# Group softmax on one core: tiles of 256 rows in six buffers, and hardware loops on VectorE and ScalarE

## The chip, the core and the metric

The kernel runs on one core of one Trainium2 chip. The metric is the device time of one execution in microseconds; lower is better. A profiled execution has a span (first to last instruction on the core) and its own time, which is a little longer.

## The reference

```python
def setup_inputs():
    B, N, D, G = 4, 4096, 4352, 8
    return {"x": np.random.randn(B, N, D).astype(np.float32)}

def reference(x):
    B, N, D = x.shape
    G = 8
    Dg = D // G
    x_g = x.reshape(B, N, G, Dg)
    x_g = x_g - x_g.max(axis=-1, keepdims=True)
    exp = np.exp(x_g)
    out = exp / exp.sum(axis=-1, keepdims=True)
    return out.reshape(B, N, D).astype(np.float32)
```

There are 16384 rows of 4352 floats. Each row is eight groups of 544, and each group gets a softmax of its own. 285 MB are read and 285 MB are written.

## The kernel before

A tile is 128 rows, one per SBUF partition, so a partition holds one row of 17408 bytes. There are 128 tiles and a pool of 12 buffers for them (`NBUF`), and everything is done in place in the buffer.

For each tile, `load` (L37) brings it in with one transfer. `expo` takes the negated maximum of all eight groups with one VectorE reduction (L45) and then runs eight ScalarE activations (L49), one per group, each of which writes exp(x - max) and leaves the group's sum. `scale` takes the reciprocals of the eight sums on VectorE (L61) and multiplies the groups with eight VectorE instructions (L63). `store` (L40) writes the tile out with one transfer.

Both kinds of transfer are issued from the SP queue[...]. The program is written out in full: there is no loop on the chip. The order is set by hand (`manual_schedule`). Ten loads are issued first (`AHEAD` is 10). Then, in step i, `expo(i)` is followed by `scale(i-1)`, `store(i-1)` and `load(i+9)`. So on VectorE the maximum of a tile stands ahead of the scaling of the tile before it. A load takes the buffer of the tile that was stored two steps earlier and waits until that store has landed. The waits between engines are placed by the Tile layer.

## Time and profile before

| | |
|---|---|
| median of 10 runs | 1341.88 us (1340.17 to 1342.72) |
| profiled execution, its own time | 1341.4 us |
| its span | 1339.6 us |
| VectorE busy | 1046.6 us (78%) |
| ScalarE busy | 764.4 us (57%) |
| moved by DMA | 570.70 MB, 426 GB/s over the span |

The profile is one execution taken by the hardware profiler. Its busy times show how much of the span an engine worked; its slices show when. The DMA lines give the mean busy share of the core's 16 DMA engines and what they moved together[...]. Queue q1 carries the kernel's loads and stores, q14 the fetching of instructions. "Landing" is when all 16 engines have reported that their share of a transfer is done.

### The profile page before, as it was taken

The numbers are of one execution on the slowest core, as the hardware profiler recorded it, in microseconds if no ns is written. First come the engines' busy times: TensorE is split into PE (matmuls) and PEld (weight loads), VectorE is DVE, ScalarE is ACT, GpSimd is POOL, SyncE is SP. The second block draws the span as 40 slices with busy tenths as digits, with TensorE's granted clock in tenths as the row PEclk, the third lists the DMA queues.
The fourth block names the chain that finished last, engine by engine and source line by source line (L and its number), as shares of the span: only waits on it lengthen the run. The fifth ranks groups of instructions, "written<-read, shape, count | busy, mean of one in ns | idle before, by whom it ended". The sixth has DMA issues, their size and how long they took to land.

```text
span 1339.6 us, 4119 instructions
## 1 busy us (share of the span) xinstructions
DVE 1046.6 (78%) x1280; ACT 764.4 (57%) x2049; POOL 0.2 (0%) x4
## 2 busy tenths in 40 slices
DVE  6999987878777877888777777778877887778760
ACT  5777766556655565556555555655555555655540
POOL 0000000000000000000000000000000000000000
DMA  9999999999999999999999999999999999999996
GB/s 399 427 429 428 431 431 432 431 430 431 432 431 430 432 431 431 431 431 431 431 430 430 431 430 431 430 431 431 431 431 430 432 431 432 430 431 431 431 431 272
DMA packets 36896, 570.70 MB, mean 426 GB/s; under 512 B 4096, under 2 KB 4096, under 8 KB 4096
## 3 DMA queue, kind: packets, MB, share of 16 engines
q1 hardware_dynamic: 36864, 570.44, 99.5%
q14 instruction: 32, 0.26, 0.0%
HBM read 285.21 MB, written 285.21 MB: 426 GB/s over the span
## 4 chain that ended last, share of the span: by engine, by line
DMA 93%; DVE 1%; SPq 1%; ACT 1%; issue 1%; DVEq 0%; ACTq 0%
DMA out_dram<-xt 91%; DMA xt<-in_x_dram 3%; SPq L37 1%; ACT xt L49 1%; DVE xt L63 1%; DVE mx L45 1%; DVE rs L61 0%; DVEq L104 0%; ACTq L104 0%
## 5 line engine op out<-in xcount | busy, mean ns | idle before, releaser
L49 ACT ACTIVATE xt<-xt,mx 128x544 f32<-128x544 f32 x1024 | 751.2, 734 | 524.1 <-issue 427.5
L45 DVE TENSOR_REDUCE mx<-xt 128x8 f32<-128x4352 f32 x128 | 599.7, 4685 | 247.2 <-DMA xt<-in_x_dram 247.1
L63 DVE TENSOR_SCALAR xt<-xt,rs 128x544 f32<-128x544 f32 x1024 | 434.1, 498 | 4.5
L49 ACT ACTIVATION_READ_ACCUMULATOR xt<-xt,mx 128x1 f32 x1024 | 191.1, 187 | 0.0
L61 DVE RECIPROCAL rs<-sm 128x8 f32<-128x8 f32 x128 | 24.7, 193 | 3.4 <-ACT xt L49 3.4
L49 ACT ACT_TABLE_LOAD x1 | 1.3, 1283 | 9.5 <-DMA xt<-in_x_dram 9.5
L93 POOL MEMSET const-bfloat16-1.0<- 128x1 bf16 x1 | 0.1, 102 | 0.0
L93 POOL MEMSET const-uint8-127<- 128x1 uint8 x1 | 0.1, 101 | 0.0
L93 POOL MEMSET const-float32-0.0<- 128x1 f32 x1 | 0.1, 99 | 0.2 <-issue 0.2
L93 POOL MEMSET const-float32-1.0<- 128x1 f32 x1 | 0.1, 98 | 0.0
## 6 DMA issues: line engine op xcount, KB each, us to landing
xt<-in_x_dram SPq DMA_DIRECT2D x128, 2176.0 KB, 25.8
out_dram<-xt SPq DMA_DIRECT2D x128, 2176.0 KB, 30.8
```

Source lines behind the costliest of these rows:

```text
L37: nc.sync.dma_start(out=xt, in_=xg[i * P:(i + 1) * P])
L45: nc.vector.reduce_max(out=mx, in_=xt, axis=mybir.AxisListType.X, negate=True)
L49: nc.scalar.activation(out=xt[:, g, :], in_=xt[:, g, :], func=mybir.ActivationFunctionType.Exp, bias=mx[:, g:g + 1], scale=1.0, accum_out= ...
L61: nc.vector.reciprocal(out=rs, in_=sums.pop(i))
L63: nc.vector.tensor_scalar_mul(out=xt[:, g, :], in0=xt[:, g, :], scalar1=rs[:, g:g + 1])
L93: nc = _bacc.Bacc("TRN2", target_bir_lowering=False, num_devices=1)
```

## The change

A tile is now 256 rows, two adjacent rows per partition (`R = 2`), so a partition's share of a transfer is one contiguous piece of 34816 bytes. There are 64 tiles in six buffers of twice the size (`NT = 6`), the same memory as before. Compute still works on 128 rows at a time, now called a row slot s of twelve (`S`): two slots per buffer, each with its own place in `mx`, `sm` and `rs`.

SP issues five loads and then alternates `store(t)` and `load(t+5)`. A load waits until the store that last used its buffer has landed. The Tile layer no longer places the waits: the kernel has semaphores of its own, `landed` and `stored` per buffer, and `max_done`, `exp_done`, `rec_done` and `scaled` across the engines. VectorE waits for its own reciprocal by `rec_done`.

VectorE and ScalarE run a hardware loop each, over a body of twelve row slots, ten turns, and the last eight row groups are written out behind it. [...] The order on VectorE is still: the maximum of the next row group, then the scaling of this one. SP's program stays written out.

```diff
-    NBUF = 12
+    R = 2
+    NT = 6
+    S = R * NT
-    nt = N // P
+    nt = N // (P * R)
+    nr = nt * R
+    turns = (nr - 1) // S
+    xt = xf.rearrange("(t p r) d -> t p (r d)", p=P, r=R)
+    ot = of.rearrange("(t p r) d -> t p (r d)", p=P, r=R)
-    pool = ctx.enter_context(tc.tile_pool(name="io", bufs=NBUF))
-    small = ctx.enter_context(tc.tile_pool(name="small", bufs=4))
+    ctx.enter_context(tc.tile_critical(no_gpsimd_drain=True))
+    ctx.enter_context(nc.cleanup_on_exit())
+    bufs = [ctx.enter_context(nc.sbuf_tensor(f"xt{b}", [P, R * D], f32)) for b in range(NT)]
...
+    def vector_max(s):
+        if s % R == 0:
+            nc.vector.sem_inc(landed[s // R], -16).wait_op(landed[s // R], 16, "sem-ge")
+        nc.vector.reduce_max(out=mx[:, s, :], in_=row(s), axis=X, negate=True).then_inc(max_done, 1)
+    def vector_scale(s):
+        nc.vector.sem_inc(exp_done, -1).wait_op(exp_done, 1, "sem-ge")
+        nc.vector.reciprocal(out=rs[:, s, :], in_=sm[:, s, :]).then_inc(rec_done, 1)
+        nc.vector.sem_inc(rec_done, -1).wait_op(rec_done, 1, "sem-ge")
+        xr = row(s)
         for g in range(G):
+            i = nc.vector.tensor_scalar_mul(
+                out=xr[:, g, :], in0=xr[:, g, :], scalar1=rs[:, s, g:g + 1])
+        i.then_inc(scaled, 1)
+    def scalar_exp(s):
+        nc.scalar.sem_inc(max_done, -1).wait_op(max_done, 1, "sem-ge")
...
+        i.then_inc(exp_done, 1)
+    def loop(engine):
+        return nc.Fori(
+            0, turns, engines=OrderedEngineSet([engine.engine]), head_slot={engine.engine: 0})
+    with nc.Block(no_gpsimd_drain=True) as block:
+        @block.sync
+        def _(sync):
+            def load(t):
+                b = t % NT
+                if t >= NT:
+                    sync.wait_ge(stored[b], 16 * (t // NT))
+                sync.dma_start(out=bufs[b][:, :], in_=xt[t]).then_inc(landed[b], 16)
-    AHEAD = NBUF - 2
-    with tc.manual_schedule():
-        for i in range(AHEAD):
-            load(i)
-        for i in range(nt + 1):
-            if i < nt:
-                expo(i)
-            if i:
-                scale(i - 1)
-                store(i - 1, nc.sync)
-                if i - 1 + AHEAD < nt:
-                    load(i - 1 + AHEAD)
+            for t in range(NT - 1):
+                load(t)
+            for t in range(nt):
+                sync.wait_ge(scaled, R * (t + 1))
+                sync.dma_start(out=ot[t], in_=bufs[t % NT][:, :]).then_inc(stored[t % NT], 16)
+                if t + NT - 1 < nt:
+                    load(t + NT - 1)
+            for b in range(NT):
+                sync.wait_ge(stored[b], 16 * ((nt - b + NT - 1) // NT))
+        @block.vector
+        def _(vector):
+            vector_max(0)
+            with loop(vector):
+                for s in range(S):
+                    vector_max((s + 1) % S)
+                    vector_scale(s)
+            for n in range(turns * S, nr):
+                if n + 1 < nr:
+                    vector_max((n + 1) % S)
+                vector_scale(n % S)
+        @block.scalar
+        def _(scalar):
+            scalar.preload_act_table(Exp)
+            with loop(scalar):
+                for s in range(S):
+                    scalar_exp(s)
+            for n in range(turns * S, nr):
+                scalar_exp(n % S)
```

## The prediction

> **What bounds the kernel now.** I read the busy line and the slices first, then the DMA queues, the chain that ended last, the groups, and last the end of the run in short windows.

> ```profile
> DVE 1046.6 (78%) x1280; ACT 764.4 (57%) x2049; POOL 0.2 (0%) x4
> ...
> DMA  9999999999999999999999999999999999999996
> GB/s 399 427 429 428 431 431 432 431 430 431 432 431 430 432 431 431 431 431 431 431 430 430 431 430 431 430 431 431 431 431 430 432 431 432 430 431 431 431 431 272
> ...
> q1 hardware_dynamic: 36864, 570.44, 99.5%
> q14 instruction: 32, 0.26, 0.0%
> ...
> DMA 93%; DVE 1%; SPq 1%; ACT 1%; issue 1%; DVEq 0%; ACTq 0%
> ```

> No compute engine is above 78%, the 16 DMA engines are full in every slice but the last, and the chain is 93% DMA. So only what makes the transfers shorter, or evens them out, moves the end. Compute has room: a row group (128 rows) costs VectorE 4.685 + 0.193 + 8 x 0.424 (434.1 us over 1024) = 8.27 us, while a load and a store of it take two transfers of 5.17 us.

> The last slice, 272 GB/s, is where the unevenness shows (columns: stretch, busy time of each engine, clock, DMA share, GB/s):

> ```profile
> 1316.00:1320.00 4.00, 0.00 (x0) 0.00 (x0) 0.00 (x0) 1.00 1.02 440
> 1320.00:1322.00 2.00, 0.00 (x0) 0.00 (x0) 0.00 (x0) 1.00 0.97 418
> 1322.00:1324.00 2.00, 0.00 (x0) 0.00 (x0) 0.00 (x0) 1.00 0.97 418
> 1324.00:1326.00 2.00, 0.00 (x0) 0.00 (x0) 0.00 (x0) 1.00 0.53 226
> 1326.00:1328.00 2.00, 0.00 (x0) 0.00 (x0) 0.00 (x0) 1.00 0.26 113
> ...
> 1332.00:1334.00 2.00, 0.00 (x0) 0.00 (x0) 0.00 (x0) 1.00 0.20 87
> 1334.00:1336.00 2.00, 0.00 (x0) 0.00 (x0) 0.00 (x0) 1.00 0.14 61
> 1336.00:1338.00 2.00, 0.00 (x0) 0.00 (x0) 0.00 (x0) 1.00 0.12 52
> ```

> One engine moves 431/16 = 27 GB/s. So all 16 work until 1324, about four at 1327, two at 1337. **The end is set by the slowest two of 16 DMA engines, some 13 us after most had finished.** The trace's completion records (one per engine and transfer) agree: of the last transfer's 16, twelve come 13.1 to 13.7 us before the last one, one 9.8, one 3.6, one 0.2. I call this distance an engine's lag. From those records the two last engines' lag grows in steps of 0.6 to 0.8 us, and most of these steps come where the packet records have one of the 28 instruction fetches (8192 bytes each) that fall inside the span: at 643.8 us one fetch, and the last lag goes from 5.8 to 6.5 us. The chain shows the same thing from outside:

> ```profile
> 478.47 30.54 DMA out_dram<-xt
> ...
> 509.40 31.55 DMA out_dram<-xt
> ...
> 541.40 30.51 DMA out_dram<-xt
> ```

> The middle piece holds two fetches, at 519.0 and 522.8 us; its neighbours hold none. Not every fetch shows (one at 450.5 fell on an engine that was not last). The two lags sum to about 27 us; 28 fetches x 0.7 = 19.6 us of it. The other 7 us come in the first 170 us and between 700 and 820 us, beside slow packets with no fetch. A third engine (9.8 us) drifts by about 0.03 us per transfer with no steps until late; I have no cause for it.

> [...] In the packet records a 17408-byte packet [...] starts 645 ns after the one before it: an overhead of 5 ns[...]. [...]

> **The change, part by part.**

> *Packets.* An engine now does, per transfer, 8 packets and a semaphore write of 9 ns: 8 x 645 + 9 = 5169 ns, x 256 = 1323.3 us (most engines in fact run from 1.75 to 1325 us). With 34816 bytes: 8 x (1280 + 5) + 9 = 10289 ns, x 128 = 1317.0 us. Saved: 6.3 us, all on the path. Bounds: 0 if the 5 ns grow with the size or the descriptor is split; 6.3 us if all of it is fixed. The jitter above 645 I leave as it is.

> *Loops.* The program goes from 1404 to 273 instructions on VectorE, from 1277 to 204 on ScalarE (2301 and 364 with the accumulator read that follows each activation) and from 398 to 155 on SP. A loop body is 152 on VectorE (12 x (1 maximum, 1 reciprocal, 8 multiplies, 2.5 waits) and the branch) and 206 on ScalarE (12 x (16 + 1 wait), and the branch). [...] so no turn should fetch. The 273 + 364 + 155 and padding are 8 to 12 fetches, mostly ahead of the first load. So of the two lags of 13.1 to 13.7 us, some 3.5 us should stay (7 us over two engines). Then the third engine is last. Its 9.8 us stay if its drift goes with bytes, and are about 5 if with packets. I take 8 us. Bounds: 3.5 (its drift gone) and 13.7 (the lag isn't the fetches). Gain 5.7 us.

> *Waits and order.* SP's queue keeps its form. load(i+5) waits for store(i-1); behind that in the ring stand load(i+4) and store(i), 2 x 10.3 us, as 4 x 5.17 us before, so an engine may lead the slowest by some 18 us before it idles; lags are below that. store(i) waits until two row groups are scaled: the second's scaling stands behind the maximum of the next tile, so it is done 4.7 + 3.6 us after load(i+1) landed; six transfers (62 us) lie between that landing and the store's place in the ring. Covered. The maximum now waits for 4.4 MB, 5.1 us more, once, at the start; five loads (51 us) are queued behind it and the first store is ready at about 14.6 + 2 x 4.7 + 7.4 + 3.4 + 3.4 = 38 us. Covered. At the end 4 stores (41 us) stand between the last landing and the last store's turn, less the lag 8; compute needs 8.3 + 4.7 + 7.4 + 3.6 = 24 us. Covered by 9 us. The own semaphores and VectorE's wait for its own reciprocal: 128 x 2.5 small instructions, none shown in the trace; at even 0.2 us each, 0.5 us per row group, they fit in VectorE's 10.3 - 8.3 = 2 us; if that cover were gone, stores would be late first. The ten branches fall there too. Bounds 0 and 2 us; I take 0.

> *Entry and exit.* One more block with its barriers, semaphore clearing: the trace has its own (first load at 0.73 us, end 0.8 us after the last landing). I take 1.6 us for a second such pair; bounds 0.5 and 4.

> **Sum** against the profiled run (span 1339.6, 1341.4 us in all): -6.3 - 5.7 + 1.6 = -10.4, so 1331.0. The median of the runs, 1341.88, is 0.5 above it: **1331.5 us**.

> **Rivals.** (a) Lag cut, packets no cheaper: 1337.8. For it: the 5 ns is small and measured only at one size. (b) Packets cheaper, lag stays since its cause is not the fetches (the stretch at 700 to 820 us speaks for that): 1341.9 - 6.3 + 1.6 = 1337.2. (c) *Slower:* the loops fetch their body again on every turn, so the change does not do what its loops are for. Two packets [...] per engine and turn are 40, with the straight code 48 fetches. At 13.5/28 us of lag each that is 23 us instead of 13.5, and the time is 1337.2 + 9.6 = 1346.8. It decides from 13.5 + 4.7 = 18.2 us of lag, or 38 fetches; there the faster engines begin to idle as well. [...] (d) Other losses: 34 KB packets slower than two of 17 KB, or a ring that runs dry at the coarser steps. If one engine in each transfer waits 0.1 us it is 128 x 0.1 = 13 us: 1344 and above. Nothing in the profile speaks for it.

> **How the numbers follow.** A measurement of this kernel can tell about 0.2% (2.7 us). Both parts work: 0.46, 1327 to 1336; with the third engine's drift gone too, 0.06, 1324 to 1327. (a) 0.13, (b) 0.09, both 1334 to 1339. No change that can be told: 0.08. (c) 0.09. (d) 0.09. Faster 0.74, same 0.08, slower 0.18. A range of 1325 to 1343 leaves out (c), (d) and a little at the low end. The likeliest case's own range is 1327 to 1336.

> **What would show it.** q14 with 12 packets or fewer, and q1 with half of its 36864; GB/s of 432 to 433 in the middle slices, where it was 431; a tail in short windows that goes from full rate to nothing in 8 us or less rather than 13; VectorE and ScalarE busy times unchanged; SP waiting for stores, not for VectorE. Wrong, if q14 has as many packets as before, if the middle slices stay at 431, or if a stretch shows the DMA share below 0.95 before the tail.

## The result and the profile after

The changed kernel takes **1331.11 us** (median of 8 runs, 1330.15 to 1332.69), the kernel before 1341.53 us (28 runs beside it). The ratio is 0.9923, 95% interval 0.9915 to 0.9932: 10.4 us faster. The forecast was 1331.5 us, and most of its steps held, but two of its terms were off in opposite directions, so that the total came out better than its parts.

From the page of the kernel after, the lines that answer to those of before:

```profile
span 1328.9 us, 4036 instructions
...
DVE 1041.4 (78%) x1280; ACT 764.5 (58%) x2049; POOL 0.2 (0%) x4
...
DMA  9999999999999999999999999999999999999997
GB/s 401 419 433 435 433 433 430 431 434 433 435 434 429 433 432 435 435 435 434 429 434 432 435 435 434 431 433 432 434 436 436 432 430 434 433 434 436 433 431 329
...
q1 hardware_dynamic: 18432, 570.43, 99.6%
q14 instruction: 9, 0.07, 0.0%
...
DVE 0%; DVEq 0%; issue 0%
```

VectorE and ScalarE do the same work in the same time. Half of the packets on q1 are gone, q14 has 9 packets where it had 32, the middle slices went from about 431 to about 433 GB/s (means of 200 us: 432 to 434, with a DMA share of 1.00 or 1.01), and the last slice from 272 to 329. The chain (last line) can no longer be read: with the kernel's own semaphores it stops after the last multiplications, so there is nothing to set beside the chain's pieces of before.

The end of the kernel after, in short windows (stretch, busy times, clock, DMA share, GB/s):

```profile
1316.00:1318.00 2.00, 0.00 (x0) 0.00 (x0) 0.00 (x0) 1.00 1.09 470
1318.00:1320.00 2.00, 0.00 (x0) 0.00 (x0) 0.00 (x0) 1.00 0.77 331
1320.00:1322.00 2.00, 0.00 (x0) 0.00 (x0) 0.00 (x0) 1.00 0.32 139
1322.00:1324.00 2.00, 0.00 (x0) 0.00 (x0) 0.00 (x0) 1.00 0.24 104
1324.00:1326.00 2.00, 0.00 (x0) 0.00 (x0) 0.00 (x0) 1.00 0.08 35
```

Before, the bulk of the engines stopped at 1324 to 1326 us and the last two went on to 1338. Now the bulk stops at 1319 to 1321 and the last at 1326. (A window's rate can exceed what the engines move, since a packet of 1.3 us is counted where it falls.) So both parts of the forecast can be seen in one view: every engine has less to do, and the spread between the engines is smaller.

To part the two in every run I take from the trace's completion records of the last transfer when the sixth of its 16 engines was done ("bulk"), and how much later the last one was ("lag"). These records carry the time of each completion and not the name of the engine, so an engine can be followed only by how far it is behind.

| kernel | time, us | ratio to before, 95% interval | bulk ends | lag | q14 packets |
|---|---|---|---|---|---|
| before | 1341.5 | | 1325.4 | 13.5 | 32 |
| after | 1331.1 | 0.9923 (0.9915 to 0.9932) | 1320.5 | 5.9 | 9 |
| e1: loops written out | 1340.6 | 0.9993 (0.9984 to 1.0001) | 1320.7 | 16.3 | 31 |
| e2: one row per partition | 1334.7 | 0.9951 (0.9937 to 0.9965) | 1325.5 | 4.9 | 10 |
| e3: both undone | 1344.0 | 1.0018 (1.0009 to 1.0026) | 1325.5 | 14.5 | 32 |
| e4: two rows, two packets | 1334.9 | 0.9953 (0.9940 to 0.9967) | 1325.0 | 5.6 | 9 |
| e5: ScalarE written out | 1336.8 | 0.9968 (0.9957 to 0.9980) | 1320.5 | 11.8 | 22 |
| e6: bodies of 24 | 1352.9 | 1.0081 (1.0068 to 1.0094) | 1323.7 | 16.8 | 32 |
| e7: bodies of 48 | 1345.4 | 1.0028 (1.0010 to 1.0045) | 1326.0 | 16.8 | 36 |
| e8: three rows | 1328.5 | 0.9901 (0.9887 to 0.9915) | 1319.0 | 5.5 | 8 |
| e9: bodies of 24, deeper ring | 1345.7 | 1.0028 (1.0017 to 1.0038) | 1335.4 | 6.4 | 33 |
| e10: transfers alone | 1330.5 | 0.9919 (0.9906 to 0.9933) | 1321.1 | 4.3 | 1 |

Bulk, lag and packets come from each kernel's one profiled execution, the times from its runs.

### The profile page after: what moved, and what is told of

Its sections match the earlier page's. It is cut to its first block, busy times and chain, and to the rows that moved or that the text cites. A ratio compares the mean times of both kernels' runs of the same rounds, so it can differ in the third digit from the quotient of the medians.

```text
span 1328.9 us, 4036 instructions
## 1 busy us (share of the span) xinstructions
DVE 1041.4 (78%) x1280; ACT 764.5 (58%) x2049; POOL 0.2 (0%) x4
## 2 busy tenths in 40 slices
DMA packets 18441, 570.51 MB, mean 429 GB/s; under 512 B 2048, under 2 KB 2048, under 8 KB 2048
```

## The experiments

### e1 to e4: each part undone

e1 writes the loops out:

```diff
-            with loop(vector):
-                for s in range(S):
-                    vector_max((s + 1) % S)
-                    vector_scale(s)
-            for n in range(turns * S, nr):
+            for n in range(nr):
                 if n + 1 < nr:
...
-            with loop(scalar):
-                for s in range(S):
-                    scalar_exp(s)
-            for n in range(turns * S, nr):
+            for n in range(nr):
                 scalar_exp(n % S)
```

> The changed kernel (1331.1 us) with its two hardware loops written out, packets of 34816 bytes kept. Theory (fetches make the lag): about 31 packets on q14 instead of 9, the last two engines' lag goes from 6 back to about 13.5 us, the packet step stays 1285 ns: 1331.1 + 7.5 = 1338.6 us. Rival (the smaller lag comes from fewer packets or transfers, not from fewer fetches): lag stays at 6 us and the time at 1331 to 1332 us.

e2 keeps the loops and goes back to one row per partition:

```diff
-    R = 2
-    NT = 6
+    R = 1
+    NT = 12
+    AHEAD = NT - 2
...
-            for t in range(NT - 1):
+            for t in range(AHEAD):
...
-                if t + NT - 1 < nt:
-                    load(t + NT - 1)
+                if t + AHEAD < nt:
+                    load(t + AHEAD)
```

> The changed kernel with its loops kept and one row per partition: 128 transfers each way of 17408-byte packets, twelve buffers, ten loads ahead as in the kernel before. Theory (a fixed 5 ns per packet and 9 ns per transfer and engine): packet step 645 ns, 6.3 us more work on every engine, lag 6 us: 1337.4 us. Rival (the whole gain is the fetches): 1331 to 1332 us.

e3 has both edits.

> Both parts undone, the own semaphores, the block and its entry and exit kept. Theory: 1331.1 + 6.3 + 7.5 = 1344.9 by the parts, which stands against 1341.5 + 1.6 = 1343.1 by the kernel before plus the second entry and exit; between 1342 and 1345 us. Rival (the own semaphores and the loop-free order bring something themselves): 1340 us or less.

e4 keeps the transfers of 4.4 MB and takes a partition's two rows from places 128 rows apart:

```diff
-    xt = xf.rearrange("(t p r) d -> t p (r d)", p=P, r=R)
-    ot = of.rearrange("(t p r) d -> t p (r d)", p=P, r=R)
+    xt = xf.rearrange("(t r p) d -> t p r d", p=P, r=R)
+    ot = of.rearrange("(t r p) d -> t p r d", p=P, r=R)
...
```

(The buffers in the two `dma_start` lines get the same shape.)

> The changed kernel with the same 64 transfers each way of 4.4 MB, but a partition's two rows lie 128 rows apart, so each is a packet of 17408 bytes. It parts what a packet costs from what a transfer costs. Theory (5 ns per packet): packet step 645 ns, 1024 x 5 = 5.1 us more per engine: 1336.2 us. Rival (the cost is the transfer's, its semaphore write and change of direction): 1331 to 1332 us.

*The loops.* Writing them out costs 9.5 us with two rows (1340.6 - 1331.1) and 9.3 us with one (1344.0 - 1334.7). The bulk does not move (1320.7 against 1320.5; 1325.5 in both), the lag does. The end of e1 in windows of 10 us shows full rate until 1320 and then one to four engines' worth of traffic until 1337:

```profile
1310.00:1320.00 10.00, 0.00 (x0) 0.00 (x0) 0.00 (x0) 1.00 0.99 428
1320.00:1330.00 10.00, 0.00 (x0) 0.00 (x0) 0.00 (x0) 1.00 0.21 91
1330.00:1340.00 10.00, 0.00 (x0) 0.00 (x0) 0.00 (x0) 1.00 0.06 28
```

The rival that the smaller lag comes from fewer packets falls: e1 keeps the large packets and has the full lag, e2 has the small ones and a small lag.

The records of e1 also tell the two late engines apart. Between 350 and 1100 us the last lag grows by 0.8 to 1.0 us about every 104 us, which is near the pace of VectorE's code; the second grows by 0.5 to 0.8 us about every 77 us, which is near ScalarE's. The paces are estimates: the page of before has 32 fetches for 4119 instructions, about 129 each, and e1 runs 1613 instructions on VectorE and 2190 on ScalarE in its span of 1339 us, so 129 in 107 us and in 79 us. So, read from these paces, each engine's code came through one late DMA engine of its own, and VectorE's fetches cost more than the 0.7 us that the prediction had taken for every fetch. That they cost more is read from this one execution and has no cause here.

*The packets.* One row instead of two costs 3.6 us with loops and 3.4 us without. Here the bulk moves: by 5.0 us (e2 against after). In the window from 1320 to 1330 us e2 still moves 259 GB/s, where e1 moved 91; and after 1330 nothing:

```profile
1310.00:1320.00 10.00, 0.00 (x0) 0.00 (x0) 0.00 (x0) 1.00 1.00 430
1320.00:1330.00 10.00, 0.00 (x0) 0.00 (x0) 0.00 (x0) 1.00 0.61 259
1330.00:1340.00 10.00, 0.00 (x0) 0.00 (x0) 0.00 (x0) 1.00 0.00 0
```

e4 parts a packet from a transfer. Its two lines of queues, beside those of after above, show what was varied: the packets are back, the transfers are not (34816 = 32768 pieces of 17408 bytes and 2048 semaphore writes; e2 has 36864).

```profile
q1 hardware_dynamic: 34816, 570.43, 99.8%
q14 instruction: 9, 0.07, 0.0%
```

Halving the transfers alone (e2 to e4) brings the bulk forward by 0.6 us (1325.52 to 1324.96) and the end not at all (1334.7 and 1334.9); halving the packets (e4 to after) brings the bulk forward by 4.5 us, or 4.4 ns for each of 1024 packets, and the end by 3.8. In the packet records the step from one packet to the next is 645 ns in e2 and e4 and 1285 ns in after, as forecast: 640 more for 17408 more bytes, which leaves 5 for the packet itself. The rival that the cost is the transfer's falls.

*Both undone.* e3 is 2.2 us slower than the kernel before (1344.0 against 1341.8 in the runs beside it), and has what that kernel has: 32 fetches, small packets. What remains between them is the block, the semaphores and the way out. From the last landing to the end of the span it takes 0.8 us before, 2.4 us in e3 and 2.5 us after; the first data packet starts 0.2 us later. These are 1.8 of the 2.2 us.

### e5 to e7: how many fetches, and where

e5 writes out ScalarE's loop alone (the second half of e1's edit).

> The changed kernel (1331.1 us) with ScalarE's loop written out and VectorE's kept: some 20 packets on q14, of which about 17 belong to ScalarE's code. Theory A (a sequencer's fetches all run on one DMA engine of its own): one engine's lag goes from 6 to 6 + 17 x 0.67 = 17 us and the others stay: 1341 us, as much as with both loops written out. Theory B (fetches are shared out over two engines): 6 + 17 x 0.67 / 2 = 11.7 us of lag: 1336.8 us. Rival (the fetches are not the cause): 1331 us.

```profile
q14 instruction: 22, 0.18, 0.0%
```

1336.8 us is theory B's number, but the completion records say A. One engine ends 11.8 us behind, the next 6.0. After 550 us ScalarE's fetches come about every 75 us, and with nearly each of them the last lag grows by 0.5 to 0.7 us, while the second stays at 6.0 from 480 us to the end: around the fetches at 1029, 1104 and 1185 us the last goes from 9.4 to 10.1, 10.7 and 11.2. With two engines served in turn the second would have grown as well. What was wrong in A's sum was its start: it put the fetches on the engine that was 6 us late anyway, and they fell on one that was not (until 480 us it is the second in the records, and then it passes the other). A number that fits is not yet the mechanism; here the shape decides.

e6 and e7 make the loop body longer, 24 or 48 row slots:

```diff
-    turns = (nr - 1) // S
+    W = 2 * S
+    turns = (nr - 1) // W
...
-                for s in range(S):
+                for s in range(W):
                     vector_max((s + 1) % S)
-                    vector_scale(s)
+                    vector_scale(s % S)
-            for n in range(turns * S, nr):
+            for n in range(turns * W, nr):
```

(likewise on ScalarE; e7 has `W = 4 * S`).

> The changed kernel with loop bodies of 24 row slots, five turns: 302 instructions on VectorE, 410 on ScalarE[...]. Theory [...]: no fetch on a turn, about 12 packets on q14, 1331 to 1332.5 us. Rival ([...] as the slower rival of the prediction had it): 5 turns of 3 and 4 packets, some 40 on q14, lag of 17 us or more, 1342 us.

> The changed kernel with loop bodies of 48 row slots, two turns and 32 row groups written out behind: 602 instructions on VectorE and 818 on ScalarE[...]. [...] about 30 packets on q14, as with no loop, lag about 14 us, 1339 to 1341 us. [...] If the time is 1331 us all the same, it is not the fetches that count.

The rival of e6 was right for ScalarE and wrong for VectorE. q14 has 32 packets where the straight program has 31, although the loops are back. The trace records the branches as well as the fetches. ScalarE's branches, at 219.8, 468.2, 718.0 and 967.8 us, are each followed by two fetches, 3 to 5 and 9 to 11 us later, and then by three at ScalarE's pace of 74 to 87 us, five in a turn. VectorE's branches, at 231.0, 480.5, 730.4 and 980.3 us, are followed by none of that kind (the one fetch within 70 us of any of them, at 761 us, is put down to SP: the kernel after has one at 756 us, and e10, without a VectorE and a ScalarE program, at 754 us). So of the two bodies ScalarE's 410 instructions were fetched anew on every turn and VectorE's 302 were not. In e7 VectorE's 602 were fetched anew as well: its branch at 480.4 us is followed by fetches at 485 and 491, ScalarE's at 469.1 by two at 474 and 479. From the page of e6:

```profile
q1 hardware_dynamic: 18432, 570.43, 98.6%
q14 instruction: 32, 0.26, 0.0%
```

And it takes more than the same number of fetches cost in e1: 1352.9 us (1344.5 to 1354.6; the profiled execution was the shortest). In e1 two engines share the fetches; in e6 those of the turns all delay one: its lag grows from 5.5 us at 260 us to 19.4 at 1270, while the second stays at 5.1 to 5.6. e7, with 36 packets, is at 1345.4 us (1338.9 to 1354.2, the widest scatter of all) where 1339 to 1341 was expected. There the page shows something new:

```profile
GB/s 400 426 430 430 434 433 433 432 430 432 431 436 436 431 431 431 433 434 434 434 431 432 431 433 438 434 431 431 431 433 436 433 433 430 431 430 418 406 434 188
```

Slices 37 and 38 (1210 to 1278 us) fall to 418 and 406 GB/s. By then the last engine is 18 to 20 us behind, about what the two transfers of 10.3 us hold that stand in the ring behind the store a load waits for. The other engines then run out of work, as the slower rival of the prediction had it, and the bulk ends at 1326.0 instead of 1320.5.

### e9: more room in the ring

e9 is e6 with four loads ahead in place of five:

```diff
...
-            for t in range(NT - 1):
+            for t in range(NT - 2):
...
-                if t + NT - 1 < nt:
-                    load(t + NT - 1)
+                if t + NT - 2 < nt:
+                    load(t + NT - 2)
```

> The loop bodies of 24 row slots again (1352.9 us, 32 packets on q14), with four loads ahead instead of five: load(t+4) then waits for store(t-2), and four transfers of 10.3 us instead of two stand in the ring behind that store. Theory (the lag of 17 to 19 us reached the end of the two transfers, so the other engines idled, on top of the lag itself): the lag may grow to 20 us but nobody idles, the other engines end at 1320.5 us as in the changed kernel: 1340 to 1342 us, and no slice under 428 GB/s before the last. Rival (the branches' waits on VectorE and ScalarE cost the 12 us over the run with all written out): 1350 us or more.

1345.7 us: 7 us better than e6, and outside both expectations. From 1200 to 1280 us e9 moves 425 to 439 GB/s, in windows of 20 us, but the room was taken from the other side: with four loads ahead, only three stores (31 us) stand between the last load and the last store. With a lag of 21 us, and by the prediction's estimate some 24 us of compute behind the last landing, the bulk waits just before the end and stops at 1335.4 us. From e9, VectorE at work (first busy time) while the DMA engines are not:

```profile
1290.00:1300.00 10.00, 6.13 (x10) 6.43 (x18) 0.00 (x0) 1.00 0.93 401
1300.00:1310.00 10.00, 8.92 (x11) 4.25 (x11) 0.00 (x0) 1.00 0.15 66
1310.00:1320.00 10.00, 7.36 (x10) 7.67 (x22) 0.00 (x0) 1.00 1.04 446
```

The expectation had looked at the ring's room and not at the slack behind the last load. That the idling is what made e6 longer than e1 fits the slices and this gain, but e6's five longest runs were not profiled, so its last 8 us are not accounted for.

### e10: what stays of the lag

All of VectorE's and ScalarE's work is taken out, and SP waits for the load:

```diff
-                sync.wait_ge(scaled, R * (t + 1))
+                sync.wait_ge(landed[t % NT], 16 * (t // NT + 1))
...
...
-        @block.vector
...
-        @block.scalar
...
```

> The changed kernel's transfers alone: all work of VectorE and ScalarE is left out, a store waits for its load instead, and the output is a copy of x. It asks where the lag of 6 us comes from that stays with the loops. Theory (the memory and the transfers themselves): the lag stays at 4 to 6 us and the time at 1329 to 1331 us. Rival (compute: its few fetches, its semaphore traffic): lag under 2 us, 1326 to 1327 us.

```profile
q14 instruction: 1, 0.01, 0.0%
```

1330.5 us, lag 4.3 us, bulk 1321.1. The transfers alone take what the whole changed kernel takes, within 0.6 us. So the compute and its few fetches cost little more than that now. The lag of 4 us grows in the first 500 us and stays; its cause in the transfers was not tried.

### e8: three rows per partition

```diff
-    R = 2
-    NT = 6
+    R = 3
+    NT = 4
...
-    nt = N // (P * R)
-    nr = nt * R
+    nr = N // P
+    nt = -(-nr // R)
...
-            for t in range(NT - 1):
+            for t in range(NT):
                 load(t)
...
-                if t + NT - 1 < nt:
+                if t and t + NT - 1 < nt:
                     load(t + NT - 1)
...
```

(the last tile has two rows per partition, and the access patterns follow it.)

> The changed kernel with three adjacent rows per partition: four buffers, 42 tiles of 384 rows and one of 256, packets of 52224 bytes, four loads ahead of the first store, then store(t) and load(t+3). Theory (4.4 ns per packet, as the lanes of the runs with one row and with two rows on different pieces give it): 341 packets less per engine, 1.5 us, and 43 x 2 instead of 128 transfers, 0.2 us: 1329.4 us. Rival (the descriptor is split, or the coarser ring runs dry at the start, in the middle or behind the last load): packets of two sizes on the page, or stretches with a DMA share under 0.95, 1333 us or more.

1328.5 us, the fastest version here: 2.6 us better than the changed kernel by the medians, against 1.7 expected. The queues of e8:

```profile
q1 hardware_dynamic: 12384, 570.43, 99.5%
q14 instruction: 8, 0.07, 0.0%
```

12384 are 43 x 2 x (128 + 16): one packet of 52224 bytes per partition (34816 in the last tile), not split. The bulk ends at 1319.0, 1.5 us earlier, as 341 packets of 4.4 ns give; the rest is 0.4 us of lag, 0.2 us at the exit and the scatter between executions.

## Why the prediction was right, and where its terms were off

**What bounds the kernel.** Right. Every kernel here ends 0.8 to 2.5 us after its last transfer has landed, and compute could be taken out (e10) with a change of 0.6 us.

**Packets: 6.3 us forecast, 5.0 measured on the bulk, 3.6 at the end.** The step of 645 to 1285 ns was exact. That of the 645 ns 640 go with the bytes and 5 do not was my estimate; the packet records of before fit it (309 ns for a fetch of 8192 bytes and 648 for a packet of 17408 are 339 ns for 9216 bytes, so 640 for 17408), and the step of after shows it. Two terms were too large: the semaphore writes (256 to 128 of 9 ns each, 1.15 us) brought 0.6 us (e4), and 5 ns per packet brought 4.4 ns over the whole run. Of the 5.0 us some were given back in these executions by a lag of 5.9 instead of 4.9 us.

**Loops: 5.7 us forecast, 9.5 measured** by e1, and 7.5 between the lags of the profiled executions before and after (13.46 to 5.92). The mechanism is shown by e1, e3 and e5, and by e6, where the loops stay and the fetches and the lag come back; the size was too low. The term that was off is the third engine: I let its 9.8 us of drift stay and took 8 us of lag. With both loops short the last engine is only 5.9 us late (after) or 4.9 (e2), and the third-latest 5.1 or 3.8. Where the rest of the third engine's lag went was not found. With one row it follows the written-out code: e2 and e3 differ by the loops alone, and their third-latest engine is 3.8 and 10.4 us behind. With two rows it doesn't: e1 is written out too, and its third-latest engine is 5.4 us behind. In these single executions it took small packets and written-out code together. I had also counted 28 fetches in the span; the page's 32 all lie in it. And e1's lag of 16.3 us, against 13.5 in the kernel before with one fetch more, shows that one price for all fetches was too simple.

**Entry and exit: 1.6 us forecast, 1.9 measured** (1.7 at the end, 0.2 at the start).

**The sum.** Against the profiles: bulk -4.9, lag -7.5, exit +1.7 is -10.7, which is what the spans differ by. The forecast's -6.3 - 5.7 + 1.6 = -10.4 came out near because the packets were 1.4 too high and the loops 1.8 too low. That two errors of this size met was luck.

**Waits and order: 0.** Right. SP's waits of the kernel after (who waited, for whom: us, times, longest):

```profile
SPq L96 <- DMA out_dram<-xt: 1139.9, 58, 20.7
SPq L102 <- DVE xt L64: 103.8, 6, 33.9
```

A load (L96) waits for a store in all 58 cases in which it must; a store (L102) waits for VectorE 6 times only. VectorE's wait for its own reciprocal shows as 1.5 us in total:

```profile
DVE mx L56 <- DVEq L55: 232.7, 56, 14.8
DVE rs L60 <- DVEq L59: 2.6, 1, 2.6
...
DVE xt L64 <- DVEq L61: 1.5, 10, 0.2
```

**The rivals.** (a) no cheaper packets: e2 and e4 say no. (b) the lag has another cause: e1 and e6 say no, for all but the 4 to 6 us that stay in e10 and in the kernel after. (c) the body is fetched on every turn: not here, since between 111 and 1243 us the packet records of the kernel after have one fetch, at 756 us, and e10, which has no VectorE and ScalarE program, has it too (754 us). But e6 shows that it is what happens to ScalarE when the body is twice as long. Its price was higher than I had put it, since the idling came on top. (d) slower packets or a ring that runs dry: 1285 ns for a packet is less than two of 645, and the means of 200 us, 432 to 434 GB/s, show no slow stretch. That no turn would fetch was my estimate. It held for bodies of 152 and 206 instructions (after), and on VectorE for 302 (e6); 410 on ScalarE (e6) and 602 on VectorE (e7) were fetched anew. Why 410 were and 302 were not is not shown here. Nor is why there are five fetches a turn in e6, where 410 instructions at about 129 each would need four.

## What to carry to other kernels

When a kernel is bound by DMA at full rate, look at its last microseconds in short windows: here the last of the 16 engines ended up to 16.8 us behind the sixth (e6, e7), and what one of them carried besides the data was on the path. A hardware loop was worth its trouble here not for the issuing engine, but because the program's own fetching takes time on a DMA engine: without the loops the lag was 16.3 us in place of 5.9, and the time 9.5 us longer (e1). Its body has to be short enough: bodies of 152 and 302 instructions on VectorE and of 206 on ScalarE stayed, 410 on ScalarE and 602 on VectorE were fetched again on the turns, and no length between was tried. And test each part of a change by undoing it: the right total here hid two terms that were off by 1.4 and 1.8 us.
